# Attention in a fixed order on TensorE: longest score rows first, transposes in shared banks, convolution taps in another place

## The chip, the cores and the metric

The program runs on one core of a Trainium2 chip. A core has TensorE (PE in the profile, with its weight loads as PEld), VectorE (DVE), ScalarE (ACT), GpSimd (POOL) and SyncE (SP), which issues most transfers. The metric is the device time of one execution in microseconds (us). Three executions of the kernel before took 2982.3, 2982.48 and 2983.72 us, median 2982.48. A difference of 0.2% is 6 us.

## The reference

Two blocks run one after the other on 512 tokens of width 1024, all in 32-bit floats. The first is a gated delta rule with pooling; the change does not touch it. The second has two layers, and in each stand a feed-forward part, a mixer, a second feed-forward part and a gate. The change lies in the mixer:

```
z = u @ w_in
y_attn = forgetting_attention(q, k, v, f_logit) @ w_attn_out
y_conv = conformer_conv(glu_in, conv_w, conv_b, g_conv) @ w_conv_out
merged = sigmoid(z_a) * y_attn + sigmoid(z_c) * y_conv
return merged @ w_out
```

The attention has 8 heads of width 64, is causal over 512 tokens in blocks of 128 queries, and adds a running sum of log-sigmoids to the scores before the softmax. The convolution is a causal one over time, channel by channel, with 31 taps on 512 channels; behind it stand an RMS normalization over the channels and a SiLU.

## The kernel before

All activations lie transposed, 128 channels by 512 tokens to a tile. A product with a weight of 32 bits is made of three matmuls on rounded halves (`mm3`, L154 to L159): high weight by high activation, high by low, low by high. The weights come in a fixed order through a stream (`Stream`, L83): a transfer of eight 128x128 blocks, then for each four blocks a rounding on ScalarE (`whi`, L108) and a subtraction on VectorE (`wlo`, L109). There are three buffers for each half, and the stream is used strictly in its order, so a projection can't begin before the one ahead of it in the order has used its weights.

The mixer of a layer runs thus. Four `glu` blocks make the inputs of the convolution (`ca`), then come the values `vt` and the forget logits. Then `heads(hp, ...)` runs for four pairs of heads (the **heads stage** below). While a pair is worked on, a filler gives TensorE the projections of the next pair's queries and keys (`qk_steps`, 16 steps of three matmuls each), for the last pair the first of the 16 gates (`first_gates`, `GATES0`, 8 steps to a gate). For a block of 128 queries (`qb`) and each of the two heads there are two score matmuls and a mask matmul into a bank `sc` (L453, L455, L459), the maximum on VectorE (L461), the exponential on ScalarE (L463), a reciprocal and a scaling on VectorE (L464, L468). Then, for each block of keys (`kb`) and each head, the rows `pe` are transposed on TensorE (L478) into a bank `pt`, copied by VectorE (L482), and multiplied with the values into `o` (L486). `split` makes `oh` and `ol` of `o` (L169, L170).

The convolution is one VectorE operation for each tap and 128 channels, 4 x 31 = 124 in a layer (L415, L420). `taps(n)` writes n of them at the place where it is called: 12 behind each `glu` block, 8 behind the values, 5 in each pair of heads (`TAPS1`), 12 behind each attention output block (`TAPS2`).

After the heads, `part(i)` for i from 0 to 7 multiplies a block of the attention output with its gate, and from 8 to 15 a block of the convolution's output; the gate for i+3 is projected ahead of it (24 matmuls to a gate, 12 to a part). `conv_out` (L563) normalizes the convolution: squares on ScalarE, sums on VectorE, one matmul for the mean (`ssps`, L261), a square root on ScalarE, then a reciprocal and three more operations on VectorE (L252 to L256), a scaling (L575), a SiLU (L576) and a split into `yh` and `yl`, which part 8 is the first to read. It is written ahead of part `CONV_AT`.

What an engine does in which order is not what the code writes: when the program is built, a list scheduler fills each engine's list. It takes the earliest instruction in the code that is ready by its own estimate, and where nothing earlier is ready it takes a later one. At run time each engine goes through its list in that order. Four banks (`acc`) hold projections, four more (`aux`) hold scores, transposes, `o` and `ssps`.

Of the kernel before, what the change touches and what calls it, by code (L numbers as in the profile page):

```python
# [7 lines left out]
F32 = mybir.dt.float32  # L8
# [5 lines left out]
P = 128  # L14
S = 512
D = 1024
KD = D // P
# [3 lines left out]
GRP = 8  # L21
UNIT = 4
AHEAD = 3
ENG2 = dict(pe="v", dup="a", pt="vv")
BANKS2 = (4, 4)
TAPS0 = 12
TAPSV = 8
GATES0 = 1
FILL = (3, 4, 3, 0, 1, 2, 1, 2)
TAPS1 = (1, 1, 2, 1)  # L30
TAPS2 = 12
CONV_AT = 5
NEG = -float(2 ** 100)
EPS = 1e-6

# [142 lines left out]
def block2(tc, kk, W, h, xp, x0, sq0, p_t, par, out_t):  # L178


    nc = tc.nc
    with ExitStack() as ctx:
# [32 lines left out]
        maskr = cp.tile([P, P], F32R, name="maskr")  # L215
# [7 lines left out]
        xh, xl = x0  # L223
# [3 lines left out]
        def mtile(i, name, dt=F32R):  # L227
            return mp.tile([P, S], dt, tag=f"m{i}", name=name)
# [37 lines left out]
        def proj(name, l, col, ps=None, k_n=KD, x=None):  # L266
            ps = psum("pj") if ps is None else ps
            x = (xh, xl) if x is None else x
            for k in range(k_n):
                w = W.get((name, l, k * P, col))  # L270
                mm3(nc, ps, w, (x[0][k], x[1][k]), k == 0, k == k_n - 1)
            return ps

        def proj_steps(ps, name, l, col):
            for k in range(KD):
                mm3(nc, ps, W.get((name, l, k * P, col)), (xh[k], xl[k]), k == 0, k == KD - 1)
                yield

        def token_sums(sq):
# [82 lines left out]
        def mixer(l, after):  # L362
# [66 lines left out]
            def taps(n):  # L429

                while n > 0 and done[0] < 31 * len(ca):
                    next(conv)
                    done[0] += 1
                    n -= 1
                if done[0] == 124:
                    next(conv, None)

            def heads(hp, qk1, filler):

                rr = [slice(64 * i, 64 * i + 64) for i in range(2)]  # L440

                def fill(n):
                    for _ in range(n):
                        next(filler, None)

                pp = [[], []]
                for qb in range(4):
                    n = (qb + 1) * P
                    qs = slice(qb * P, qb * P + P)
                    pss = [paux("sc") for i in range(2)]  # L450
                    for i, ps in enumerate(pss):
                        q, k = qk1[i]
                        nc.tensor.matmul(ps[:, :n], lhsT=q[:, qs], rhs=k[:, :n], start=True, stop=False)  # L453
                        q, k = qk2[hp % 2][i]
                        nc.tensor.matmul(ps[:, :n], lhsT=q[:, qs], rhs=k[:, :n], start=False, stop=False)  # L455
                    fill(FILL[qb])
                    for i, ps in enumerate(pss):
                        o = ps[:, :n]
                        nc.tensor.matmul(ps[:, qs], lhsT=kk.identr, rhs=maskr, start=False, stop=True)  # L459
                        sm = sp.tile([P, 4], F32, tag="sm", name="sm", bufs=4)  # L460
                        nc.vector.tensor_reduce(sm[:, 0:1], o, axis=mybir.AxisListType.X, op=ALU.max, negate=True)  # L461
                        pe = cp.tile([P, n], F32, tag=f"pe{qb}", name="pe", bufs=2)
                        nc.scalar.activation(pe, o, AF.Exp, bias=sm[:, 0:1], accum_out=sm[:, 1:2])  # L463
                        nc.vector.reciprocal(sm[:, 2:3], sm[:, 1:2])  # L464
                        if ENG2["pe"] == "a":
                            nc.scalar.activation(pe, pe, AF.Copy, scale=sm[:, 2:3])
                        else:
                            nc.vector.tensor_scalar(pe, pe, sm[:, 2:3], None, op0=ALU.mult)  # L468
                        pp[i].append(pe)
                    taps(TAPS1[qb])  # L470
                po_ = paux("o")
                for kb in range(4):
                    n = S - kb * P
                    pts = []
                    for i in range(2):
                        ps = paux("pt")
                        for qb in range(kb, 4):
                            nc.tensor.transpose(ps[:, (qb - kb) * P:(qb - kb) * P + P], pp[i][qb][:, kb * P:kb * P + P],  # L478
                                                kk.ident)
                        t = mtile(8 + kb % 2 * 4 + 2 * i, "pt", F32)[:, :n]  # L480
                        copy = nc.scalar.copy if ENG2["pt"][i] == "a" else nc.vector.tensor_copy
                        copy(t, ps[:, :n])  # L482
                        pts.append(t)
                    fill(FILL[4 + kb])
                    for i, r in enumerate(rr):
                        nc.tensor.matmul(po_[r, kb * P:], lhsT=vt[kb][:, hp * P + 64 * i:hp * P + 64 * i + 64], rhs=pts[i],  # L486
                                         start=kb == 0, stop=kb == 3)
                split(nc, oh[hp], ol[hp], po_)

            for cb in range(4):  # L490
# [11 lines left out]
            for k in range(KD):  # L502
                wh, wl = W.get(("w_in_2", l, k * P, 1024), 4)
# [5 lines left out]
            vt = [mtile(t, f"vt{t}", F32) for t in range(4)]  # L509
# [20 lines left out]

            gates = []

            def gate_steps(i):
                pg = psum("pj")
                yield from proj_steps(pg, "w_in_2", l, 2568 + i * P)
                g = tmp("ga")
                nc.vector.tensor_tensor(g, pg, R, op=ALU.mult)
                nc.scalar.activation(g, g, AF.Sigmoid)
                gates.append(g)

            def gate(i):
                for _ in gate_steps(i):
                    pass

            def first_gates():
                for i in range(GATES0):
                    yield from gate_steps(i)

            qk1 = [], []
            for _ in qk_steps(0, qk1):  # L550
# [54 lines left out]
            for m in range(KD):  # L605
                ps = proj("w_out_2", l, m * P, x=(mh, ml))
# [37 lines left out]
        v = sp.tile([P, 4], F32, name="lv")  # L644
        r = sp.tile([P, 4], F32, name="lr")
# [3 lines left out]
        for m in range(KD):  # L649
            t = tmp("fin")  # L650
# [950 lines left out]
```

## Time and profile before

| | |
|---|---|
| median of three runs | 2982.48 us |
| the profiled execution | 2981.43 us, of it span 2979.7 us |
| PE busy | 2934.9 us (98%) |
| DVE busy | 1910.1 us (64%) |
| ACT busy | 1298.3 us (44%) |
| layer 1, heads stage, 1174.8 to 1267.7 us | 92.90 us: PE busy 89.50, DVE 83.90, ACT 52.76 |
| layer 1, 1267.7 to 1341.0 us, up to part 8 | 73.30 us: PE busy 73.30, DVE 62.44, ACT 33.10 |
| layer 2, heads stage and a little, 2292.2 to 2385.6 us | 93.40 us: PE busy 90.21, DVE 83.31, ACT 52.87 |

A row of the instruction view has the start, the duration, the engine, the line, the operation, what it writes and reads, and in brackets how long the engine stood idle before it and what ended that. A matmul's start is measured, its end is modelled, and one begins before the last has ended: the distance from start to start tells TensorE's pace. VectorE's operations overlap a little in the records too.

### The profile page before, as it was taken

How to read it: one execution, taken by the hardware profiler on the slowest of the kernel's cores; microseconds unless marked ns; L12 is line 12 of the kernel's file. 1: busy time of each engine (PE TensorE's matmuls, PEld its weight loads, DVE VectorE, ACT ScalarE, POOL GpSimd, SP SyncE). 2: the span in 40 equal slices, each digit the busy share in tenths (PEclk: the TensorE clock that was granted, in tenths of full speed). 3: DMA queues.
4: the chain of work that ended last, by engine and by line, in shares of the span. 5: the costliest groups of instructions: out<-in, count | busy, mean ns of one | idle time of the engine just before them, and what ended most of it. 6: DMA issues, size and time to landing. Idle time of an engine off the chain costs nothing.

```text
span 2979.7 us, 37937 instructions
## 1 busy us (share of the span) xinstructions
PE 2934.9 (98%) x13992; PEld 2392.2 (80%) x13992; DVE 1910.1 (64%) x3753; ACT 1298.3 (44%) x2387; POOL 48.1 (2%) x105
## 2 busy tenths in 40 slices
PE   8999999999999999999999999999999999999998
PEld 5888887778888887688888888888888688888886
DVE  6788888787544469886543447444469886543446
ACT  6567766435323335544432335323335544432333
POOL 1000000000000000000000000000000000000000
PEclk9999999999999999999999999999999999999999
DMA  5211123233233332123333333333232123233332
GB/s 216 57 42 47 45 58 106 92 92 92 92 99 98 94 99 85 50 85 99 94 98 99 96 95 102 97 99 98 94 99 84 50 87 99 92 99 98 94 99 85
DMA packets 112986, 268.77 MB, mean 90 GB/s; under 512 B 43552, under 2 KB 47136, under 8 KB 112800
## 3 DMA queue, kind: packets, MB, share of 16 engines
q1 hardware_dynamic: 111776, 266.28, 28.8%
q8 instruction: 110, 1.80, 0.2%
q14 instruction: 76, 0.62, 0.1%
q0 software_dynamic: 1024, 0.07, 0.0%
HBM read 262.17 MB, written 4.06 MB: 89 GB/s over the span
## 4 chain that ended last, share of the span: by engine, by line
PE 93%; DVE 3%; ACT 2%; issue 1%; DMA 0%; SPq 0%; DVEq 0%; ACTq 0%
PE pj L158 17%; PE pj L157 17%; PE pj L159 17%; PE fo L158 5%; PE fo L157 5%; PE fo L159 5%; PE px L157 3%; PE px L158 3%; PE px L159 2%; PE o L486 1%; PE wo L158 1%; PE mX L1285 1%; PE wo L159 1%; PE mP L1290 1%; PE wo L157 1%; PE chn L1337 1%
## 5 line engine op out<-in xcount | busy, mean ns | idle before, releaser
L108 ACT CAST whi<-wraw 128x512 fp32r<-128x512 f32 x914 | 567.1, 621 | 1163.9 <-PE pj L158 699.3
L109 DVE TENSOR_TENSOR wlo<-wraw,whi 128x512 fp32r<-128x512 f32 x914 | 627.3, 687 | 446.1 <-ACT whi L108 423.6
L158 PE MATMUL pj<-xl,whi 128*128 128x512 f32 x1712 | 672.6, 393 | 0.0
L157 PE MATMUL pj<-xh,whi 128*128 128x512 f32 x1712 | 670.5, 392 | 0.9 <-DVE h L1526 0.9
L159 PE MATMUL pj<-xh,wlo 128*128 128x512 f32 x1712 | 669.3, 391 | 0.0
L159 PEld LDWEIGHTS pj<-xh,wlo 128*128 128x128 f32 x1712 | 321.9, 188 | 67.9 <-issue 2.3
L158 PEld LDWEIGHTS pj<-xl,whi 128*128 128x128 f32 x1712 | 322.2, 188 | 66.9 <-issue 2.7
L157 PEld LDWEIGHTS pj<-xh,whi 128*128 128x128 f32 x1712 | 322.2, 188 | 66.4 <-ACT whi L108 1.3
L157 PE MATMUL fo<-gh,whi 128*128 128x512 f32 x704 | 273.9, 389 | 0.0
L158 PE MATMUL fo<-gl,whi 128*128 128x512 f32 x704 | 273.9, 389 | 0.0
L159 PE MATMUL fo<-gh,wlo 128*128 128x512 f32 x704 | 273.9, 389 | 0.0
L420 DVE SCALAR_TENSOR_TENSOR cy<-ca,par,cy 128x489 f32<-128x489 f32 (+17 forms) x240 | 169.6, 729 | 1.5
L157 PE MATMUL px<-xh,whi 128*128 128x512 f32 x392 | 160.3, 409 | 0.8 <-ACT xh L1000 0.7
L158 PE MATMUL px<-xl,whi 128*128 128x512 f32 x392 | 160.6, 410 | 0.0
L159 PE MATMUL px<-xh,wlo 128*128 128x512 f32 x392 | 159.1, 406 | 0.0
L157 PEld LDWEIGHTS fo<-gh,whi 128*128 128x128 f32 x704 | 132.1, 188 | 27.5
L159 PEld LDWEIGHTS fo<-gh,wlo 128*128 128x128 f32 x704 | 132.1, 188 | 27.5
L158 PEld LDWEIGHTS fo<-gl,whi 128*128 128x128 f32 x704 | 132.1, 188 | 27.4
L341 DVE TENSOR_TENSOR fb<-pj,R 128x512 f32<-128x512 f32 x88 | 60.8, 691 | 129.9 <-PE pj L159 129.9
L338 DVE TENSOR_TENSOR fa<-pj,R 128x512 f32<-128x512 f32 x88 | 60.8, 691 | 125.4 <-PE pj L159 123.5
L157 PE MATMUL pj<-nh,whi 128*128 128x512 f32 x352 | 137.3, 390 | 0.0
L158 PE MATMUL pj<-nl,whi 128*128 128x512 f32 x352 | 137.0, 389 | 0.0
(427 smaller groups left out, 4473.4 us busy)
## 6 DMA issues: line engine op xcount, KB each, us to landing
wraw<-in_w_dram SPq DMA_DIRECT2D x465, 512.0 KB
mw<-in_w_dram SPq DMA_DIRECT2D x16, 512.0 KB
raw<-in_xt_dram SPq DMA_DIRECT2D x8, 256.0 KB
h<-in_xt_dram SPq DMA_DIRECT2D x8, 256.0 KB
out_dram<-fin SPq DMA_DIRECT2D x8, 256.0 KB
db<-B SPq DMA_DIRECT2D x64, 6.0 KB
Pm<-dq SPq DMA_DIRECT2D x64, 12.0 KB
Qm<-dq SPq DMA_DIRECT2D x64, 12.0 KB
```

What stands on the lines that cost most here:

```text
L108: nc.scalar.copy(hi, src)
L109: nc.vector.tensor_tensor(lo, src, hi.bitcast(F32), op=ALU.subtract)
L157: nc.tensor.matmul(ps, lhsT=wh, rhs=xh, start=start, stop=False)
L158: nc.tensor.matmul(ps, lhsT=wh, rhs=xl, start=False, stop=False)
L159: nc.tensor.matmul(ps, lhsT=wl, rhs=xh, start=False, stop=stop)
L338: nc.vector.tensor_tensor(a, pa, R, op=ALU.mult)
L341: nc.vector.tensor_tensor(b, pb, R, op=ALU.mult)
L420: nc.vector.scalar_tensor_tensor(yy[:, s:], ca[cb][:, :S - s], pcol("conv_w", l, cb, j), yy[:, s:], op0=ALU.mult, op1=ALU.add)
L486: nc.tensor.matmul(po_[r, kb * P:], lhsT=vt[kb][:, hp * P + 64 * i:hp * P + 64 * i + 64], rhs=pts[i], start=kb == 0, stop=kb == 3)
L1285: nc.tensor.matmul(pX[:, o], lhsT=st.B[:, m0 + m], rhs=alt(st.Q, m0 + m), start=True, stop=True)
L1290: nc.tensor.matmul(pP[:, o], lhsT=Xt[:, m], rhs=alt(st.P, m0 + m), start=True, stop=True)
L1337: nc.tensor.matmul(pa, lhsT=st.kN[:, c], rhs=y2, start=True, stop=True)
```

## The change

Scores: the query blocks go from the last (512 keys) to the first (128 keys), and the three matmuls of a head stand together, with the filler's steps behind each block (`FILL`). Softmax: the scaling of the second head's rows moves to ScalarE (`ENG2`). Transposes: five batches instead of eight, each filling a bank of 512 columns, copied in turn by VectorE and ScalarE; three batches, two filler steps, the values of key block 0, two batches, two filler steps, and the values of key blocks 1 to 3, both heads each time. All these matmuls, and the filler's, are marked to stay in the order in which the code writes them (`keep_in_program_order`). The calls of `taps` inside `heads` are gone, `conv_out` is written ahead of part 7 instead of part 5, and the last pair has two gates as its filler instead of one. No transfer is added, taken away or moved: the lists of POOL and SP are the same.

```diff
-ENG2 = dict(pe="v", dup="a", pt="vv")
+ENG2 = dict(pe="va", dup="a", pt="vavav")
-GATES0 = 1
-FILL = (3, 4, 3, 0, 1, 2, 1, 2)
-TAPS1 = (1, 1, 2, 1)
+GATES0 = 2
+FILL = (2, 2, 3, 5, 2, 2)
-CONV_AT = 5
+CONV_AT = 7
...
+        def pin(*a, **kw):
+            tc.keep_in_program_order(nc.tensor.matmul(*a, **kw))
...
-                for qb in range(4):
+                for qi, qb in enumerate((3, 2, 1, 0)):
...
-                        if ENG2["pe"] == "a":
+                        if ENG2["pe"][i] == "a":
...
-                    taps(TAPS1[qb])
+                    fill(FILL[qi])
+                banks = (((0, 0),), ((1, 0),), ((0, 1), (0, 3)), ((1, 1), (1, 3)), ((0, 2), (1, 2)))
+                def transposes(j):
+                    ps = paux("pt")
+                    t = mtile(8 + (5 * hp + j) % 8, "pt", F32)
...
+                    copy = nc.scalar.copy if ENG2["pt"][j] == "a" else nc.vector.tensor_copy
+                    copy(t[:, :at], ps[:, :at])
+                def values(kb):
+                    for i, r in enumerate(rr):
+                        pin(po_[r, kb * P:], lhsT=vt[kb][:, hp * P + 64 * i:hp * P + 64 * i + 64], rhs=pts[kb][i],
+                            start=kb == 0, stop=kb == 3)
+                for j in range(3):
+                    transposes(j)
+                fill(FILL[4])
+                po_ = paux("o")
+                values(0)
+                for j in range(3, 5):
+                    transposes(j)
+                fill(FILL[5])
+                for kb in range(1, 4):
+                    values(kb)
```

**TensorE's list, the values of the first pair of heads in layer 1.** `pj` is a projection of the filler, `pt` a transpose, `o` a product with the values. Before:

```order
L486 MATMUL o<-pt,vt_10929 64x512 x2
L478 MATMUL pt<-ident,pe 128x128 x8
L159 MATMUL pj<-xh_10175,wlo 128x512
L157 MATMUL pj<-xh_10233,whi 128x512
L158 MATMUL pj<-xl_10234,whi 128x512
L486 MATMUL o<-pt,vt_10930 64x384
L478 MATMUL pt<-ident,pe 128x128 x2
L159 MATMUL pj<-xh_10233,wlo 128x512
L486 MATMUL o<-pt,vt_10930 64x384
```

And now:

```order
L276 MATMUL o<-pt,vt_10929 64x512 x2
L488 MATMUL pt<-ident,pe 128x128 x8
L276 MATMUL pj<-xh_10347,whi 128x512
L276 MATMUL pj<-xl_10348,whi 128x512
L276 MATMUL pj<-xh_10347,wlo 128x512
L276 MATMUL pj<-xh_10399,whi 128x512
L276 MATMUL pj<-xl_10400,whi 128x512
L276 MATMUL pj<-xh_10399,wlo 128x512
L276 MATMUL o<-pt,vt_10930 64x384 x2
L276 MATMUL o<-pt,vt_10931 64x256 x2
L276 MATMUL o<-pt,vt_10932 64x128 x2
L276 MATMUL sc<-qk_11295,qk_11204 128x512
```

The two heads' products of a key block now stand side by side, in two runs to a pair instead of six, and the next pair's scores come right behind the second.

**VectorE's list, the end of the first pair of heads in layer 1.** `cy` is a tap of the convolution, `ol` the low half of the pair's output, with which a pair ends. Before:

```order
L109 TENSOR_TENSOR wlo<-wraw,whi 128x512
L482 COPY pt<-pt 128x384
L482 COPY pt<-pt 128x256 x2
L482 COPY pt<-pt 128x128
L420 SCALAR_TENSOR_TENSOR cy<-ca,par_80,cy 128x482
L482 COPY pt<-pt 128x128
L420 SCALAR_TENSOR_TENSOR cy<-ca,par_80,cy 128x504
L415 TENSOR_SCALAR cy<-ca,par_80 128x512
L170 TENSOR_TENSOR ol_10419<-o,oh_10415 128x512
```

And now:

```order
L109 TENSOR_TENSOR wlo<-wraw,whi 128x512
L493 COPY pt<-pt 128x512 x2
L427 SCALAR_TENSOR_TENSOR cy<-ca,par_80,cy 128x500
L427 SCALAR_TENSOR_TENSOR cy<-ca,par_80,cy 128x510
L427 SCALAR_TENSOR_TENSOR cy<-ca,par_80,cy 128x499
L427 SCALAR_TENSOR_TENSOR cy<-ca,par_80,cy 128x509
L493 COPY pt<-pt 128x512
L427 SCALAR_TENSOR_TENSOR cy<-ca,par_80,cy 128x498
L109 TENSOR_TENSOR wlo<-wraw,whi 128x512
L384 SCALAR_TENSOR_TENSOR qk<-pj,R 128x512
L427 SCALAR_TENSOR_TENSOR cy<-ca,par_80,cy 128x497
L170 TENSOR_TENSOR ol_10419<-o,oh_10415 128x512
```

The scheduler has set taps between the copies; over the four pairs of a layer, from behind the first pair's last `qk` scaling to the last `ol`, the list holds 59 taps where it held 26, and behind that none, where it held 33.

**TensorE's list, from the mean of the convolution's squares to part 8.** `ssps` is that mean, the rows with `xh` and `xl` are a gate, `yh` is what part 8 reads. Before, the list from the mean on began thus:

```order
L261 MATMUL ssps<-ysq,ones_74 128x512
L158 MATMUL pj<-xl_10234,whi 128x512
L159 MATMUL pj<-xh_10233,wlo 128x512
L157 MATMUL pj<-xh_10289,whi 128x512
L158 MATMUL pj<-xl_10290,whi 128x512
```

And now it ends thus ahead of part 8:

```order
L159 MATMUL pj<-xh_10289,wlo 128x512
L157 MATMUL pj<-xh_10347,whi 128x512
L158 MATMUL pj<-xl_10348,whi 128x512
L159 MATMUL pj<-xh_10347,wlo 128x512
L157 MATMUL pj<-xh_10399,whi 128x512
L158 MATMUL pj<-xl_10400,whi 128x512
L159 MATMUL pj<-xh_10399,wlo 128x512
L157 MATMUL pj<-yh_12520,whi 128x512
L158 MATMUL pj<-yl_12524,whi 128x512
```

Between the mean and the first matmul with `yh` stood 83 matmuls (the rest of a gate, part 6, a gate, part 7, a gate); now there stand 11, the rest of one gate. Layer 2 has the same lists.

## Rows read from the trace of the kernel before

**Rows 1.** Page, busy time, share and instructions of each engine.

```profile
PE 2934.9 (98%) x13992; PEld 2392.2 (80%) x13992; DVE 1910.1 (64%) x3753; ACT 1298.3 (44%) x2387; POOL 48.1 (2%) x105
```

**Rows 2.** Stretches: length; busy PE, PEld, DVE, ACT, POOL (instructions); PEclk, DMA, GB/s.

```profile
1175.70:1269.10 93.40, 90.56 (x435) 61.87 (x436) 83.83 (x198) 53.05 (x118) 3.83 (x8) 0.98 0.18 52
1267.70:1341.00 73.30, 73.30 (x323) 60.11 (x322) 62.44 (x93) 33.10 (x52) 0.00 (x0) 1.00 0.28 87
2292.20:2385.60 93.40, 90.21 (x426) 61.44 (x424) 83.31 (x197) 52.87 (x118) 4.47 (x10) 0.96 0.17 52
```

**Rows 3.** VectorE by line, 1175.7 to 1269.1: busy, mean ns, idle before.

```profile
L420 DVE SCALAR_TENSOR_TENSOR cy<-ca,par,cy 128x485 f32<-128x485 f32 (+24 forms) x25 | 17.9, 724 | 0.1
L482 DVE COPY pt<-pt 128x512 f32<-128x512 f32 (+3 forms) x32 | 14.5, 485 | 4.2 <-PE pt L478 3.9
L468 DVE TENSOR_SCALAR pe<-pe,sm 128x128 f32<-128x128 f32 (+3 forms) x32 | 11.3, 379 | 0.0
L170 DVE TENSOR_TENSOR ol<-o,oh 128x512 fp32r<-128x512 f32 x4 | 2.8, 690 | 1.9 <-ACT oh L169 1.9
```

**Rows 4.** The same with shapes apart, the widest copy.

```profile
L482 DVE COPY pt<-pt 128x512 f32<-128x512 f32 x8 | 5.3, 683 | 0.3
```

**Rows 5.** TensorE in order of time, where the heads stage begins.

```profile
1174.53 0.39 PE L157 MATMUL pj<-xh,whi 128*128 128x512 f32 x1
1174.76 0.39 PE L158 MATMUL pj<-xl,whi 128*128 128x512 f32 x1
1177.15 0.33 PE L453 MATMUL sc<-qk,qk 128*128 128x128 f32 x1 [2.01 <-ACT qk L395]
```

**Rows 6.** TensorE in order of time, products with the values (two records each).

```profile
1196.10 0.86 PE L486 MATMUL o<-pt,vt 128*64 128x384 f32 x2
...
1263.98 0.87 PE L486 MATMUL o<-pt,vt 128*64 128x384 f32 x4
...
1267.33 0.44 PE L486 MATMUL o<-pt,vt 128*64 128x128 f32 x4
```

**Rows 7.** TensorE in order of time, the convolution's mean and part 8.

```profile
1321.41 1.10 PE L261 MATMUL ssps<-ysq,ones 128*128 128x512 f32 x2
1321.94 0.80 PE L158 MATMUL pj<-xl,whi 128*128 128x512 f32 x1
1322.58 0.40 PE L159 MATMUL pj<-xh,wlo 128*128 128x512 f32 x1
...
1341.21 0.39 PE L157 MATMUL pj<-yh,whi 128*128 128x512 f32 x1
```

**Rows 8.** VectorE in order of time, from the mean to the scaled outputs.

```profile
1323.72 3.35 DVE L253 RECIPROCAL R<-rs 128x512 f32<-128x512 f32 x1 [1.31 <-ACT rs L252]
1326.99 0.63 DVE L109 TENSOR_TENSOR wlo<-wraw,whi 128x512 fp32r<-128x512 f32 x1
...
1331.57 0.68 DVE L256 SCALAR_TENSOR_TENSOR R<-rs,R 128x512 f32<-128x512 f32 x1
1332.17 0.68 DVE L586 TENSOR_TENSOR ma<-pj,ga 128x512 f32<-128x512 f32 x1
1332.77 1.40 DVE L575 SCALAR_TENSOR_TENSOR cy<-cy,par,R 128x512 f32<-128x512 f32 x2
```

**Rows 9.** ScalarE in order of time, the same stretch.

```profile
1323.00 0.69 ACT L252 ACTIVATE rs<-ssps,epsb 128x512 f32<-128x512 f32 x1
...
1335.01 1.15 ACT L576 ACTIVATE cy<-cy 128x512 f32<-128x512 f32 x2
...
1336.58 1.14 ACT L169 CAST yh<-cy 128x512 fp32r<-128x512 f32 x2
```

**Rows 10.** Stretches behind the wait of rows 5, columns as in rows 2.

```profile
1178.00:1180.00 2.00, 1.61 (x11) 1.57 (x10) 1.97 (x5) 1.67 (x2) 0.00 (x0) 0.75 0.78 262
1180.00:1182.00 2.00, 2.00 (x8) 1.81 (x7) 2.00 (x9) 1.86 (x8) 0.00 (x0) 0.50 0.00 0
2299.00:2301.00 2.00, 2.00 (x7) 1.85 (x6) 1.83 (x8) 2.00 (x7) 0.00 (x0) 0.50 0.01 4
```

More of the change, by code (lines that the diff above doesn't have):

```diff
@@ L272, in proj @@
             return ps
+        def pin(*a, **kw):
+            tc.keep_in_program_order(nc.tensor.matmul(*a, **kw))
         def proj_steps(ps, name, l, col):
             for k in range(KD):
-                mm3(nc, ps, W.get((name, l, k * P, col)), (xh[k], xl[k]), k == 0, k == KD - 1)
+                (wh, wl), x = W.get((name, l, k * P, col)), (xh[k], xl[k])
+                pin(ps, lhsT=wh, rhs=x[0], start=k == 0, stop=False)
+                pin(ps, lhsT=wh, rhs=x[1], start=False, stop=False)
+                pin(ps, lhsT=wl, rhs=x[0], start=False, stop=k == KD - 1)
                 yield
@@ L444, in fill @@
                         next(filler, None)
-                pp = [[], []]
-                for qb in range(4):
+                pp = [[None] * 4, [None] * 4]
+                for qi, qb in enumerate((3, 2, 1, 0)):
                     n = (qb + 1) * P
                     qs = slice(qb * P, qb * P + P)
-                    pss = [paux("sc") for i in range(2)]
-                    for i, ps in enumerate(pss):
+                    for i in range(2):
+                        ps = paux("sc")
+                        o = ps[:, :n]
                         q, k = qk1[i]
-                        nc.tensor.matmul(ps[:, :n], lhsT=q[:, qs], rhs=k[:, :n], start=True, stop=False)
+                        pin(o, lhsT=q[:, qs], rhs=k[:, :n], start=True, stop=False)
                         q, k = qk2[hp % 2][i]
[L455 to L459, printed above, removed]
+                        pin(o, lhsT=q[:, qs], rhs=k[:, :n], start=False, stop=False)
+                        pin(ps[:, qs], lhsT=kk.identr, rhs=maskr, start=False, stop=True)
                         sm = sp.tile([P, 4], F32, tag="sm", name="sm", bufs=4)
@@ L468, in heads @@
                             nc.vector.tensor_scalar(pe, pe, sm[:, 2:3], None, op0=ALU.mult)
-                        pp[i].append(pe)
-                    taps(TAPS1[qb])
-                po_ = paux("o")
[L472 to L487, printed above, removed]
+                        pp[i][qb] = pe
@@ new lines, in heads @@
+                    fill(FILL[qi])
+                pts = [[None, None] for _ in range(4)]
+                banks = (((0, 0),), ((1, 0),), ((0, 1), (0, 3)), ((1, 1), (1, 3)), ((0, 2), (1, 2)))
+                def transposes(j):
+                    ps = paux("pt")
+                    t = mtile(8 + (5 * hp + j) % 8, "pt", F32)
+                    at = 0
+                    for i, kb in banks[j]:
+                        n = S - kb * P
+                        for qb in range(kb, 4):
+                            o = at + (qb - kb) * P
+                            tc.keep_in_program_order(nc.tensor.transpose(ps[:, o:o + P], pp[i][qb][:, kb * P:kb * P + P],
+                                                                         kk.ident))
+                        pts[kb][i] = t[:, at:at + n]
+                        at += n
+                    copy = nc.scalar.copy if ENG2["pt"][j] == "a" else nc.vector.tensor_copy
+                    copy(t[:, :at], ps[:, :at])
@@ L531, in mixer, with open_gate @@
             gates = []
-            def gate_steps(i):
-                pg = psum("pj")
-                yield from proj_steps(pg, "w_in_2", l, 2568 + i * P)
+            def open_gate(pg):
                 g = tmp("ga")
@@ L541, in gate @@
             def gate(i):
-                for _ in gate_steps(i):
-                    pass
+                open_gate(proj("w_in_2", l, 2568 + i * P))
             def first_gates():
+                pgs = []
                 for i in range(GATES0):
-                    yield from gate_steps(i)
+                    pgs.append(psum("pj"))
+                    yield from proj_steps(pgs[i], "w_in_2", l, 2568 + i * P)
+                for pg in pgs:
+                    open_gate(pg)
             qk1 = [], []
```

## The prediction

> **What bounds the kernel now.** I read the page's first part first: TensorE is busy for 98% of the span and VectorE for 64% [rows 1]. So what counts is where TensorE waits or works slowly, and whether the change makes it wait anew. Then the stretches of one mixer [rows 2]. From 1267.7 us, behind the heads, to 1341.0 TensorE is busy for all of 73.30 us: nothing can be won there, only lost. In the heads stage VectorE is busy for 83.83 of 93.40 us, 90%, far more than its share of the span. TensorE has one long wait there, 2.01 us for ScalarE at the start of the first pair [rows 5]. So the heads stage is a place where two engines stand close to their limits, and a change that relieves TensorE wins only as far as VectorE follows. Then VectorE by line in the stage [rows 3], for what the change takes from it and gives to it; then, in order of time, the chain from the mean of the convolution's squares to part 8 on TensorE, VectorE and ScalarE [rows 7 to 9]; last the granted clock behind a wait [rows 10].
>
> **The heads stage, TensorE's side.** The number of score, mask, transpose and value matmuls stays, and so does that of projections, but for the second gate, which comes earlier and is missing later: no work is added. What becomes cheaper is the pairing of the two heads. One head's product of 384 columns took 0.86 us alone; where both heads' stood side by side, the two together took 0.87 [rows 6]. In the list before, 6 of a layer's 16 products stand apart (in the first pair of heads those of 384 and 128 columns), 1664 columns in all, 1664/384 x 0.86 = 3.7 us; now all 16 stand side by side. TensorE was idle for 2.84 us [rows 2], 2.01 of them in rows 5, so 0.8 us of other waits may go. That is 4.5 us in each layer; what the fewer changes between kinds of matmuls save has no row of its own, and I let it be as much again at most, so 4.5 to 9 us. The wait at the start stays: the first pair's queries and keys come no sooner.
>
> **The heads stage, VectorE's side.** This decides. From behind the first pair's last query and key scaling to the last `ol` VectorE's list held 197 instructions and now holds 193. Taken away: 32 copies at a mean of 0.485 us, 15.5 us, for which 12 of full width at 0.683 come, 8.2 [rows 3, 4], so -7.3; 16 of 32 scalings at 0.379 [rows 3], -6.1; one weight subtraction, -0.6 [rows 8]. Added: 59 - 26 = 33 taps at 0.724 [rows 3], +23.9. Sum: +9.9 us. The taps that the code puts behind the heads stand, in the list that the scheduler made, inside them, since it fills every moment in which it believes VectorE idle.
>
> VectorE was busy for 83.83 us in this stretch [rows 2], so it now has 93.7 us of work there, as much as the whole stage lasted. What TensorE needs of it is the last copy of transposes in the fourth pair, five rows ahead of the end (a tap, a weight subtraction, a gate, a tap, `ol`): they are 5 x 0.61 = 3.0 us, leaving 90.7. Without a single idle moment this copy is done at 1175.7 + 90.7 = 1266.4. The last products with the values follow, three pairs of at most 0.87 us [rows 6], about 1.7 us: 1268.1. Before, the last ones ended with the row at 1267.33, and TensorE's next matmul started at 1267.70 [rows 2, 6]. By then it now has done five projections more, 5 x 0.227 = 1.1 us by the distance of the starts in rows 5. So with VectorE never idle the stage is 0.7 us better than before. It won't be idle never: it waited 9.6 us of 93.40, of that 3.9 for transposes and 1.9 for `oh` [rows 2, 3]. The copies are now fewer and later, the wait for `oh` stays; I take 1.7 us of idle time, near the second figure. That gives **+1.0 us in a layer**.
>
> The ends: busy time counts the last 0.08 us of each operation even where the next starts later (a 0.68 us operation starts 0.60 behind its like [rows 8]), which may make 3.3 us, so -4; and if it stands idle as long as before, 9.6 us, +8.9. The nearest row is the wait for `oh`, hence +1.0.
>
> ScalarE gets 16 scalings and 8 copies, at 0.6 us at most 14 us on 53.05 [rows 2], 67 of 93: it can follow, and I put nothing for it.
>
> **Part 8 and the convolution's norm.** In the list before, 83 matmuls, 18.8 us, stand between the mean of squares and the first matmul with `yh`; that first one starts 19.8 us behind the mean, without an idle moment [rows 7]. Now 11 stand there. Count from the mean's start, T. TensorE: the next matmuls start at T + 0.53 and T + 1.17 [rows 7], ten more distances of 0.227 end at T + 3.4, where part 8 wants to start. The chain: square root at T + 1.59 [rows 7, 9]; reciprocal at T + 2.31, and what follows on VectorE 3.27 us later, T + 5.58 [rows 8]. In the new list a weight subtraction, an operation, a gate's product and two operations come there, at 0.60 each and 0.67 where one needs the one before: the first scaled output starts at T + 8.7, is done at T + 9.4, and ScalarE's SiLU starts at T + 9.5. Two SiLUs take 1.1 us, the rounding to `yh` 0.6 [rows 9]: part 8 starts at T + 11.2. TensorE stands idle for 7.8 us. Then it is paced by the rest: two more SiLUs and roundings, and the four `yl`, put the last operand at T + 14.6, part 8 ends at T + 15.1 instead of T + 6.2. **Loss: 8.9 us in a layer**, and nothing gives it back, since TensorE is full before and behind.
>
> The ends: without the weight subtraction and the gate in VectorE's chain 7.3 us; with the chain as slow as before (`yh` first rounded by 1337.2, T + 15.8 [rows 7, 9]) 13.
>
> **The clock.** After the wait of 2.01 us [rows 5] the granted clock fell to 0.75 and then 0.50 of full while TensorE was busy for 2.00 of 2.00 us, so to the lower of its levels, 1.2 of 2.4 GHz; in layer 2, whose stage begins ahead of 2292.2 [rows 2], it was 0.50 between 2299 and 2301 with TensorE busy throughout [rows 10]. Part 8's 12 matmuls at half pace cost 12 x 0.227 = 2.7 us more, of which about 1.2 lie inside the waits for `yl`. I add **1.5 us in a layer** (0 to 3).
> [...]
>
> **The other edits.** The reversed order of query blocks frees the banks of the long rows late and those of the short ones early; behind each block stand 6 to 15 projections, 1.4 to 3.4 us, and the banks come free with the exponentials, about as long after the scores: nothing. No transfer moves. The second gate needs a second projection bank, of four, while no other is wanted: nothing.
>
> **Sum.** For each layer +1.0 + 8.9 + 1.5 = 11.4 us, for two +22.8. The profiled execution took 2981.43 us (its span 2979.7 and 1.7 around it), the median is 1.05 above it. 2981.4 + 22.8 = 3004.2, at the median's level **3005 us**, 0.8% slower.
>
> **Rivals.**
> *TensorE sets the heads' pace (not slower).* The taps fit into moments in which VectorE idles, and TensorE wins its whole 9 us in each layer. For it: TensorE waited little in the stage, and the scheduler, too, laid the taps into idle moments of its own reckoning. Against it: even with the distances shortened as far as the -4 above allows, VectorE has no room for more than half. With -9 + 10.4 a layer is 1.4 us slower: 2985, no measurable change; with the low end of the wait at part 8 (7.3, no clock) it is 1.7 faster, 2979. It decides from 4 us in a layer.
> *The chain to part 8 is hidden.* Part 8's wait would need cover that the list doesn't hold. TensorE would have to take other matmuls first, against its list. Then +1.0 to -4 in a layer: 2984 to 2974.
> *More waits and a colder clock.* VectorE as the bound leaves TensorE idle in each heads stage for the 4.5 to 9 us that it saves, in small pieces, while it waits for weights and copies; if the clock is low for 15 us more of the stage and VectorE idles as much as before, a layer costs up to 8.9 + 8.9 + 3 = 21: 3018 to 3025.
> *The change doesn't do what it says.* Half of this is in the forecast already: the taps are not behind the heads.
>
> **Chances.** Forecast (2993 to 3015) 0.68; colder and more idle 0.15; TensorE's pace 0.11; chain hidden 0.06. The range for 8 in 10 runs from 2989, where the -4 in the heads and 7.3 at part 8 meet (2 x 3.3 and the median's level), to 3019. Faster or slower means by over 0.2%, 6 us, about what a measurement of this kernel can tell from no change: faster 0.05, same 0.10 (most of the first rival and half of the second), slower 0.85.
>
> **What would show it.** Part 8: a gap of about 8 us on TensorE right ahead of the first matmul with `yh`, ended by ScalarE's `yh`, in both layers, with the granted clock at 0.50 behind it; without it the forecast is wrong by 20 us. Heads: VectorE busy for over 92% from the first score to the last `ol`, TensorE waiting for VectorE's weight halves and copies several times in each pair, the two heads' products side by side in all 16 places. If TensorE's heads stage ends more than 4 us earlier than before, VectorE was not the bound there. Outside the mixers nothing should differ.

## The result and the profile after

The changed kernel took 3019.06 us (median of four executions, 3016.27 to 3020.72) against 2982.74 for the kernel before in the same comparison: ratio 1.0121, interval 1.0109 to 1.0133, 36 us slower. Forecast were 3005 us and a range of 2989 to 3019. The direction was right, the size was 1.6 times the forecast, and the time lies at the range's end (3019.06 against 3019). The profiled execution, the slowest of the four, took 3020.72 us, 39.3 more than the profiled one before; 1.8 of that stand ahead of the first mixer.

The page's busy line, to be held against [rows 1]:

```profile
PE 2934.8 (97%) x13992; PEld 2402.0 (80%) x13992; DVE 1887.7 (63%) x3681; ACT 1317.0 (44%) x2431; POOL 48.1 (2%) x105
```

TensorE's busy time is the same to 0.1 us. All the loss is idle time or work at half pace that replaced work at full pace elsewhere. TensorE's waits over the whole program (waiter, what released it, us in total, times, longest):

```profile
PE sc L276 <- ACT qk L402: 24.7, 14, 6.5
PE pj L157 <- ACT yh L169: 17.6, 2, 8.8
```

The first was 4.6 us in all before the change, the second did not exist. The stretches that answer to [rows 2], from the first score to behind the last product with the values, first in layer 1 before the change, then in layers 1 and 2 after it, and from there to the mean of the convolution's squares:

```profile
1177.15:1267.70 90.55, 89.16 (x430) 60.69 (x430) 81.57 (x194) 51.20 (x115) 3.83 (x8) 0.98 0.18 53
1178.93:1273.97 95.04, 87.59 (x437) 66.01 (x437) 89.98 (x189) 59.77 (x136) 3.83 (x8) 0.94 0.16 45
2315.92:2410.78 94.86, 87.45 (x438) 65.78 (x438) 90.08 (x189) 59.77 (x136) 3.83 (x8) 0.94 0.15 45
1273.97:1346.70 72.73, 72.73 (x322) 59.98 (x320) 31.77 (x49) 25.30 (x42) 0.00 (x0) 1.00 0.31 95
```

VectorE is busy for 95% of the heads stage and TensorE idle for 7.5 us of it; before, for 1.4. In the dense stretch nothing is lost, and VectorE has little to do there now. TensorE in order of time, where the stage begins (answers to [rows 5]) and where the second and third pairs of heads begin:

```profile
1172.00 0.39 PE L276 MATMUL pj<-xh,wlo 128*128 128x512 f32 x1
1178.93 0.79 PE L276 MATMUL sc<-qk,qk 128*128 128x512 f32 x1 [6.54 <-ACT qk L402]
...
1203.45 0.50 PE L276 MATMUL sc<-qk,qk 128*128 128x512 f32 x1 [2.02 <-ACT qk L402]
...
1228.49 0.50 PE L276 MATMUL sc<-qk,qk 128*128 128x512 f32 x1 [1.84 <-ACT qk L402]
```

The first score stands no later than before, 44.9 us behind the layer's first matmul of the values in both. But 20 projections that TensorE did ahead of it before are now held behind it, so the wait is 4.5 us longer. Each later pair's first scores wait for the last split of keys by ScalarE (the fourth pair's for 1.4 us). The way there on VectorE and on ScalarE at the end of the first pair:

```profile
1199.58 0.68 DVE L493 COPY pt<-pt 128x512 f32<-128x512 f32 x1
1200.18 0.73 DVE L427 SCALAR_TENSOR_TENSOR cy<-ca,par,cy 128x498 f32<-128x498 f32 x1
1200.82 0.68 DVE L109 TENSOR_TENSOR wlo<-wraw,whi 128x512 fp32r<-128x512 f32 x1
1201.42 0.68 DVE L384 SCALAR_TENSOR_TENSOR qk<-pj,R 128x512 f32<-128x512 f32 x1
```

```profile
1202.14 0.62 ACT L389 CAST qk<-qk 64x512 fp32r<-64x512 f32 x1
1202.78 0.62 ACT L402 CAST qk<-qk 64x512 fp32r<-64x512 f32 x1
```

The keys' last projection matmul had started at 1199.60; a tap and a weight subtraction stand ahead of its scaling, then come two casts. Between the projection and the scores TensorE's fixed list has only six products with the values (two records each).

At part 8 (answers to [rows 7 to 9]), TensorE, VectorE and ScalarE:

```profile
1346.74 1.10 PE L261 MATMUL ssps<-ysq,ones 128*128 128x512 f32 x2
...
1349.97 0.39 PE L159 MATMUL pj<-xh,wlo 128*128 128x512 f32 x1
1359.16 0.79 PE L157 MATMUL pj<-yh,whi 128*128 128x512 f32 x1 [8.80 <-ACT yh L169]
...
1364.74 0.63 PE L157 MATMUL pj<-xh,whi 128*128 128x512 f32 x1
```

```profile
1349.04 3.35 DVE L253 RECIPROCAL R<-rs 128x512 f32<-128x512 f32 x1 [1.31 <-ACT rs L252]
...
1355.50 2.74 DVE L598 SCALAR_TENSOR_TENSOR cy<-cy,par,R 128x512 f32<-128x512 f32 x4
```

```profile
1354.21 1.28 ACT L558 ACT_TABLE_LOAD   x1 [3.43 <-DVE ga L557]
1355.51 0.63 ACT L558 ACTIVATE ga<-ga 128x512 f32<-128x512 f32 x1
1356.15 1.28 ACT L599 ACT_TABLE_LOAD   x1
1357.45 1.15 ACT L599 ACTIVATE cy<-cy 128x512 f32<-128x512 f32 x2
1358.51 1.12 ACT L169 CAST yh<-cy 128x512 fp32r<-128x512 f32 x2
```

With T = 1346.74 the scaling starts at T + 8.76 as forecast (T + 8.7). The SiLU starts at T + 10.71 instead of T + 9.5: the gate's sigmoid stands ahead of it on ScalarE, and each of the two has a table load of 1.28 us. The sigmoid is through when the first scaled output is ready, at about 1356.15; the SiLU's own load, from 1356.15 to 1357.43, is what the chain gained. Part 8 is followed at T + 18.0; forecast were T + 15.1 and 1.5 us of clock. Its twelve matmuls, most of them started 0.43 us apart where 0.227 is usual, ran at the lower level, as the clock column says (stretches behind the wait at part 8 and behind the three waits ahead of scores shown above):

```profile
1359.10:1364.00 4.90, 4.84 (x11) 3.53 (x12) 2.59 (x4) 2.61 (x6) 0.00 (x0) 0.50 0.00 0
1178.93:1182.00 3.07, 3.07 (x8) 2.29 (x9) 2.95 (x5) 2.86 (x4) 0.00 (x0) 0.50 0.00 0
1204.00:1207.00 3.00, 2.82 (x8) 2.18 (x9) 2.89 (x5) 1.50 (x5) 0.00 (x0) 0.65 0.00 0
1229.00:1232.00 3.00, 2.62 (x12) 2.01 (x13) 2.86 (x5) 1.50 (x5) 0.00 (x0) 1.00 0.02 5
```

**One measure for all runs.** Kernels differ in how many projections TensorE has done by the end of the heads. So I take the time from a layer's first matmul of the values (`vt`) to the last product with them, less 0.2275 us for each projection matmul in between: the *heads' cost*. Before, layer 1: from 1132.22 to 1267.49 with 281 projections, 135.27 - 63.93 = 71.3. After: from 1134.00 to 1273.77 with 269, 139.77 - 61.20 = 78.6. The same way from the mean to the first matmul with `yh` less the projections between is 0.9 before and 9.9 after: the wait at part 8 costs 9.0. From there to the next norm's mean, less the projections, it is -0.2 before and 3.1 after: 3.3 more, part 8 at half pace.

The measure holds the clock too. The changed kernel and e2 below run the same instructions in the same order in the heads, and layer 2 costs 78.4 and 80.3 (mean granted clock of the stage 0.94 and 0.91); so do e4 and e5, and layer 1 costs 68.5 and 66.7 (0.96 and 1.00). A difference of under 2 us between two runs therefore says nothing about their lists.

### The profile page after: what moved, and what is told of

Its sections match the earlier page's. It is cut to its first block, busy times and chain, and to the rows that moved or that the text cites. A ratio compares the mean times of both kernels' runs of the same rounds, so it can differ in the third digit from the quotient of the medians.

```text
span 3019.0 us, 37821 instructions
## 1 busy us (share of the span) xinstructions
PE 2934.8 (97%) x13992; PEld 2402.0 (80%) x13992; DVE 1887.7 (63%) x3681; ACT 1317.0 (44%) x2431; POOL 48.1 (2%) x105
## 4 chain that ended last, share of the span: by engine, by line
PE 93%; DVE 3%; ACT 3%; issue 1%; DMA 0%; SPq 0%; DVEq 0%; ACTq 0%
PE pj L157 16%; PE pj L158 16%; PE pj L159 16%; PE fo L157 5%; PE fo L159 5%; PE fo L158 5%; PE pj L276 3%; PE px L157 3%; PE px L158 3%; PE px L159 2%; PE wo L158 1%; PE mX L1308 1%; PE wo L159 1%; PE sc L276 1%; PE mP L1313 1%; PE wo L157 1%
## 5 line engine op out<-in xcount | busy, mean ns | idle before, releaser
L158 PE MATMUL pj<-xl,whi 128*128 128x512 f32 x1552 | 607.2, 391 | 0.0
L157 PE MATMUL pj<-xh,whi 128*128 128x512 f32 x1552 | 605.0, 390 | 0.9 <-DVE h L1549 0.9
L159 PE MATMUL pj<-xh,wlo 128*128 128x512 f32 x1552 | 604.1, 389 | 0.0
L159 PEld LDWEIGHTS pj<-xh,wlo 128*128 128x128 f32 x1552 | 291.4, 188 | 62.8 <-issue 2.3
L158 PEld LDWEIGHTS pj<-xl,whi 128*128 128x128 f32 x1552 | 291.6, 188 | 62.0 <-issue 1.9
L157 PEld LDWEIGHTS pj<-xh,whi 128*128 128x128 f32 x1552 | 291.6, 188 | 61.8 <-ACT whi L108 1.3
L427 DVE SCALAR_TENSOR_TENSOR cy<-ca,par,cy 128x489 f32<-128x489 f32 (+21 forms) x240 | 169.5, 729 | 1.0
```

The costliest lines, as they stand in the source:

```text
L427: nc.vector.scalar_tensor_tensor(yy[:, s:], ca[cb][:, :S - s], pcol("conv_w", l, cb, j), yy[:, s:], op0=ALU.mult, op1=ALU.add)
```

## The experiments

All times are medians; the kernel before took 2980.8, 2981.5 and 2981.9 us beside the three groups of runs (e1 to e4, e5 to e8, e9 to e12). Heads' costs are those of layers 1 and 2.

| run | us | ratio to before, interval | heads' cost | PE idle ahead of part 8 |
|---|---|---|---|---|
| before | 2982.7 | | 71.3, 72.6 | none |
| after | 3019.1 | 1.0109 to 1.0133 | 78.6, 78.4 | 8.8 |
| e1 before, norm ahead of part 7 | 3004.4 | 1.0066 to 1.0096 | 71.4, 71.7 | 8.8 |
| e2 after, norm ahead of part 5 | 2998.4 | 1.0042 to 1.0072 | 78.5, 80.3 | none |
| e3 after, taps held behind the heads | 3006.5 | 1.0068 to 1.0098 | 72.0, 71.7 | 9.3 |
| e4 after, filler 8 steps ahead | 2997.7 | 1.0040 to 1.0074 | 68.5, 68.5 | 8.8 |
| e5 e4 and norm ahead of part 5 | 2973.0 | 0.9964 to 0.9983 | 66.7, 66.7 | none |
| e6 e5 and taps dealt out | 2995.7 | 1.0030 to 1.0059 | 79.1, 79.2 | none |
| e7 after, no marks, norm ahead of part 5 | 2965.9 | 0.9930 to 0.9960 | 65.4, 63.7 | none |
| e8 before, `ENG2` shared | 2978.3 | 0.9978 to 0.9996 | 70.4, 70.2 | none |
| e9 after, no marks | 2993.9 | 1.0023 to 1.0049 | 67.1, 65.2 | 8.8 |
| e10 e7 with filler ahead | 2969.9 | 0.9949 to 0.9975 | 66.0, 66.0 | none |
| e11 e7, short rows first | 2971.1 | 0.9957 to 0.9980 | 67.4, 67.0 | none |
| e12 e7, VectorE alone | 2970.7 | 0.9948 to 0.9974 | 66.0, 65.2 | none |

**e1 and e2: part 8 alone.** The kernel before with `-CONV_AT = 5` `+CONV_AT = 7`, and the changed kernel with the opposite edit.

> The kernel before with one number changed: the convolution's norm is written ahead of part 7 instead of part 5. TensorE's list then has 11 matmuls between the mean of squares and part 8, as in the changed kernel, and 83 stood there before; the heads are as before. Theory (part 8's wait is a loss of its own, with nothing to pay it back): in each layer 9.0 us of waiting ahead of part 8, as between the two profiled executions, and 3.2 us for part 8 at the lower clock, 12.2 a layer, 2982.7 + 24.4 = 3007 us. Rival (the wait needs the changed heads, since they push the convolution's end): the wait is under 3 us and the time under 2990.

> The changed kernel with the convolution's norm written ahead of part 5 again; 83 matmuls stand between the mean and part 8. Theory (two losses that add up): part 8's 12.2 us a layer go, the heads keep theirs, 7.2 us in layer 1 and 5.8 in layer 2: 3019.1 - 24.4 = 2995 us, with 6.5 us of waiting ahead of the first score and three waits of about 2 us ahead of the other pairs' first scores as they were. Rival (the wait at part 8 comes from VectorE being late out of the heads, so it stays): above 3010. Rival that the heads cost nothing by themselves: 2983.

Measured: +23.6 us and -20.7. In e1 TensorE's longest new wait is the same as in the changed kernel, with heads like those before:

```profile
1349.33 0.79 PE L157 MATMUL pj<-yh,whi 128*128 128x512 f32 x1 [8.79 <-ACT yh L169]
```

Against the kernel before that ran beside each, e1 lost 23.6 us and e2 17.6. Together that is 41.2 where the changed kernel lost 36.3, so the two losses add up to within 5 us; 1.9 of the 5 are the clock in e2's second layer. Part 8 costs 9 to 12 us a layer by itself, and the heads the rest.

**e3: VectorE without taps in the heads.**

```diff
-                    taps(TAPS2)
+                    with tc.issue_after(last[0].ins):   # last: the last pair's `ol` on VectorE
+                        taps(TAPS2)
```

The `taps(200)` ahead of the norm is held in the same way.

> The changed kernel with all taps that the code writes behind the heads held behind the last pair's low half on VectorE: 0 taps in the heads stage instead of 56, 68 behind it instead of 0. Theory V (VectorE's work holds the heads): without 56 x 0.725 = 40 us VectorE is no longer full; the three waits of about 2 us ahead of the pairs' first scores shrink below 1 us, and the heads stage from the first score to the last product falls from 95 us to 85 to 90. Theory O (the fixed order holds them: a pair's first scores stand right behind the projection that its keys come from, so the wait is the latency of scaling, split and copy whatever VectorE has beside it): the three waits stay at 1.5 to 2.2 us, the stage shrinks by less than 3 us. In both the wait ahead of part 8 stays or grows (2 matmuls of cover instead of 11, VectorE with 68 taps there): 9 to 14 us a layer. Time by V 2998 to 3012, by O 3015 to 3025.

Measured: 3006.5 us, the heads' cost down by 6.6 and 6.7. The time (2998 to 3012) and the length of the stage (85 to 90 us) are those of theory V, and theory O's were missed; but of the waits at the pairs, which by V go below 1 us each, 5.2 of 5.8 us in layer 1 are left. The stage:

```profile
1177.18:1266.96 89.78, 84.40 (x436) 65.13 (x436) 59.03 (x133) 61.80 (x137) 4.00 (x9) 0.94 0.15 48
```

VectorE is down to 59 of 90 us, yet TensorE still waits for ScalarE's keys at each pair, now 0.64 and 1.09 us for the two heads (1.7 together; 2.02 and 0.18 at the second pair of the changed kernel). So taking the taps out, which make each answer of VectorE later, won back most of what the heads had lost (72.0 and 71.7 are left, the kernel before had 71.3 and 72.6). But with not one tap in the stage the waits at the pairs are still there: they belong to the order.

**e4 and e5: the keys projected earlier.**

```diff
+            def ahead():
+                for hp in range(1, 4):
+                    yield from qk_steps(hp, nxt[hp])
+                yield from first_gates()
+            filler = ahead()
+            for _ in range(8):
+                next(filler)
```

All pairs share this filler, `FILL` is (2, 2, 3, 3, 2, 2); e5 has `CONV_AT = 5` too.

> The changed kernel with the filler made one stream that runs 8 steps ahead: 24 projections of the second pair stand ahead of the first score, and each pair's keys are projected half a pair before its first scores; matmuls in fixed order as before, norm ahead of part 7 as in the changed kernel. Theory O: the waits ahead of the pairs' first scores (4.5 us more than before at the first, three of about 2 us) go, and the half-paced stretches behind them; 6 to 10 us a layer, 2999 to 3007 us. Theory V: VectorE's list is nearly as long (47 taps in the stage instead of 56), so TensorE's idle time in the stage only moves to other waits (copies of transposes, weights) and stays over 5 us; what is won is the start and 9 taps, 3 to 5 us a layer, 3009 to 3013. In both the wait of about 9 us ahead of part 8 stays.

> The run with the leading filler and, besides, the norm ahead of part 5 again. Theory (the two losses add up): part 8's wait of 9.0 us and its half-paced matmuls, 2.8, go in each layer: 2997.7 - 23.6 = 2974 us, below the kernel before. Rival (without the wait at part 8 VectorE's work of the convolution is late elsewhere): 2978 to 2985.

Measured: 2997.7 and 2973.0 us. Theory O's figure was exceeded: 10 us a layer, with 47 taps still in the stage. The waits ahead of later pairs' first scores are gone. But theory V's sign came true as well: TensorE's idle time moved to other waits, now ahead of the transposes for the scaled rows, and was 6.5 us in e4's stage and 7.4 in e5's. The stages of the two, and the longest waits in e4's:

```profile
1176.29:1263.79 87.50, 80.98 (x425) 61.38 (x425) 83.43 (x178) 61.56 (x138) 3.84 (x8) 0.96 0.16 49
1176.58:1262.28 85.70, 78.31 (x425) 59.00 (x425) 83.23 (x178) 61.46 (x138) 3.84 (x8) 1.00 0.16 50
```

```profile
PE pt L489 <- DVE pe L474: 2.8, 1, 2.8
PE pt L489 <- ACT pe L472: 2.4, 2, 2.2
```

Of the 10 us in layer 1, 24 x 0.2275 = 5.5 are projections done ahead of a first score that came no later, and 0.9 less idle time; the rest is matmuls that took less time, at a mean granted clock of 0.96 instead of 0.94. With the early norm it beats the kernel before.

**e6: the taps dealt out.** e5 with two taps behind each block of scores, held behind the maximum of the block's second head (`red` is the last one set), the rest held behind the heads:

```diff
                     fill(FILL[qi])
+                    with tc.issue_after(red.ins):
+                        taps(2)
```

> The same with the taps dealt out: 2 behind each block of scores and held behind the first maximum (32 taps in the heads stage instead of 47), the other 36 held behind the last pair, and only 56 instead of 67 ahead of the first score. Theory V (VectorE's work still sets the stage's length with the leading filler): the first score comes 1.8 us sooner, as with the taps held behind, and 2 to 3 us more go in the stage: 7 to 10 us less than the run with leading filler and early norm, 2964 to 2967. Theory O (the order was the cause and the lead has settled it): within 4 us of that run, 2970 to 2976.

Both theories missed: 2995.7 us, 22.7 slower than e5, with fewer taps in the stage (32 for 47). The stage, and TensorE's waits in it:

```profile
1173.67:1273.00 99.33, 84.00 (x424) 64.03 (x424) 75.13 (x165) 61.19 (x138) 4.01 (x8) 0.91 0.13 43
```

```profile
PE pt L492 <- DVE pe L475: 9.7, 2, 5.2
PE pt L492 <- ACT pe L473: 3.1, 1, 3.1
```

VectorE is busy for 76%, and TensorE is idle for 15.3 us, more than in any other run. The taps, which by their place in the code now come ahead of work written later, stand between a row's maximum and its scaling; in the second pair, ahead of the wait of 5.2 us, there are eight of them. In the first pair:

```profile
1184.97 0.40 DVE L468 TENSOR_REDUCE sm<-sc 128x1 f32<-128x256 f32 x1
1185.29 0.71 DVE L428 SCALAR_TENSOR_TENSOR cy<-ca,par,cy 128x484 f32<-128x484 f32 x1
1185.92 0.41 DVE L468 TENSOR_REDUCE sm<-sc 128x1 f32<-128x256 f32 x1
1186.26 0.15 DVE L471 RECIPROCAL sm<-sm 128x1 f32<-128x1 f32 x1
1186.33 0.70 DVE L428 SCALAR_TENSOR_TENSOR cy<-ca,par,cy 128x483 f32<-128x483 f32 x1
1186.95 0.34 DVE L475 TENSOR_SCALAR pe<-pe,sm 128x256 f32<-128x256 f32 x1
```

So the amount of VectorE's work doesn't decide by itself: what stands ahead of the one operand that the fixed list needs next can cost more than a smaller amount saves.

**e7 and e9: the marks taken off.**

```diff
         def pin(*a, **kw):
-            tc.keep_in_program_order(nc.tensor.matmul(*a, **kw))
+            nc.tensor.matmul(*a, **kw)
```

The same for the transposes. e7 has `CONV_AT = 5`, e9 has 7 and is the changed kernel but for the marks.

> The changed kernel without the marks that hold TensorE's order (the code's order, banks and engines as in the changed kernel) and with the norm ahead of part 5. TensorE's list has 20 projections ahead of the first score again, 36 taps stand in the heads stage instead of 56. If the fixed order is what costs in the heads, their cost falls by 6 to 8 us a layer, to that of the kernel before: 2998.4 - 14 = 2984 us. If the order of the rows and the shared banks cost, whatever holds them: 2994 to 3000. If these gain and only the fixed order loses: below 2977.

> The changed kernel with the marks that hold TensorE's order taken off and nothing else; the norm stays ahead of part 7, with 11 matmuls between the mean and part 8. If the marks' loss and part 8's add up, it takes what the unmarked kernel with the early norm took and 11.8 us more in each layer: 2965.9 + 23.6 = 2989.5 us. If the gain in the heads were eaten by the convolution, which now has 21 taps behind the heads, the wait ahead of part 8 would be longer than 9.0 us and the time above 2995.

Measured: 2965.9 us for e7, the fastest of all, 0.55% below the kernel before; its third case came true. The stage, and TensorE's waits in it:

```profile
1175.01:1255.50 80.49, 78.90 (x410) 59.60 (x412) 77.11 (x168) 58.57 (x136) 3.84 (x8) 0.96 0.16 53
```

```profile
PE sc L276 <- ACT qk L402: 2.0, 1, 2.0
PE o L276 <- DVE pt L492: 0.9, 2, 0.8
```

VectorE is busy for 77.11 of 80.49 us, 96%, a larger share than after the change, and TensorE idles for 1.6. Its list holds 36 taps in the stage where the changed kernel's held 56, 77 us of work for 90. The products of the two heads stand side by side here too. e9, which differs from the changed kernel by the marks alone, is 25 us faster than it, and its heads' cost is 11.5 and 13.2 lower. It is 4.4 us above its figure, between its two cases; the wait at part 8 is the same 8.8 us, and 3.2 of the 4.4 are in the heads, with the lists of e7 there.

**e8 and e10 to e12: what else is in it.** e8 is the kernel before with `ENG2 = dict(pe="va", dup="a", pt="va")` and `ENG2["pe"][i]`. The others are e7 with the stream of e4, with `enumerate((0, 1, 2, 3))`, and with `ENG2 = dict(pe="vv", dup="a", pt="vvvvv")`.

> The kernel before with the second head's scalings and copies of transposes on ScalarE instead of VectorE, nothing else (no fixed order; the scheduler sets 41 taps into the heads stage instead of 23, and 15 instead of 33 behind it). If VectorE's work sets the pace of the heads stage before the change, TensorE's wait there shrink and it is 4 to 8 us faster, 2973 to 2977. If not (VectorE stood idle for 9.6 us of that stage, and TensorE for 1.4 behind the first score), it is within 3 us of the kernel before, 2978 to 2984; more taps in the stage eat what the scalings leave.

> The unmarked kernel with the norm ahead of part 5 and, besides, the filler as one stream 8 steps ahead. If the lead only repairs what the fixed order spoils (a pair's keys projected right ahead of its first scores), nothing is left for it here: 2963 to 2969 us. If the lead has a worth of its own (the wait of 2.0 us ahead of the first score goes, and the half-paced stretch behind it), 2 to 4 us a layer more: 2958 to 2962.

> The unmarked kernel with the norm ahead of part 5, but the score rows from the shortest to the longest, as in the kernel before. If the order of the rows is worth nothing: within 4 us of 2965.9. If a good part of what this kernel has over the one before (15.6 us) is the order of the rows: 2972 or more, with TensorE waiting for the exponentials of the last, longest rows ahead of the first transposes.

> The unmarked kernel with the norm ahead of part 5, but all scalings and copies on VectorE, as before the change: 16 scalings and 8 copies a layer, some 11.6 us, go back to it, and the scheduler sets 21 taps instead of 36 into the heads stage. If relieving VectorE is what wins: 4 to 6 us a layer are lost, 2974 to 2978. If the shared banks and the products side by side win: within 4 us of 2965.9, since the taps make room.

Measured: 2978.3, 2969.9, 2971.1 and 2970.7 us. e8 wins 3.2 us, at the edge of its second case. It doesn't show what less work on VectorE is worth, since the scheduler set taps in the place of the scalings and VectorE was as busy as before (82.2 us in the stage for 81.6). No gain from the lead is seen without the marks (1 us above the range of its first case). e11 and e12 lie between their two cases. In the heads' cost the order of the rows makes 2.0 and 3.3 us a layer and the sharing with ScalarE 0.6 and 1.5, less than the 6 and 9 that e7 has over the kernel before, but hardly more than the 2 us that the clock can make, and the intervals of e10, e11 and e12 overlap that of e7. What is left is owed to what these runs share: the banks, the products side by side, the second gate, the other places of filler and taps. None was undone alone, so their shares stay open.

## Why the prediction was right in direction and short in size

*Part 8 and the norm: the mechanism right, 2 us short in a layer.* Forecast were 8.9 us, of them 7.8 idle ahead of part 8 and 1.1 waits inside it, and 1.5 of clock, 10.4 in all. Measured are 9.0 ahead of it and 3.3 inside (3.2 in layer 2), 12.3 in all. The chain came as worked out up to the scaled output; the idle time was 8.8 instead of 7.8 us, since the table load ahead of the SiLU was not in the sum. The kernel before had it there too (from 1333.72), and [rows 8, 9] show that the SiLU began 1.5 us behind the first scaled output and not 0.1. Part 8 itself waited hardly at all for `yl`, but all twelve matmuls and the next ones ran at half pace: the estimate that 1.2 of 2.7 us would lie inside other waits was wrong. The granted clock was 0.50 behind this wait, 0.65 behind the wait of 2.02 us and 1.00 behind that of 1.84. The Trainium skill ("TensorE: Matmul & The Clock Gate", section "HAM oscillation — how this bites in real kernels") describes a kernel in which each burst follows a wait for a transfer of about 3 to 5 us and starts cold. The trace agrees for the wait of 8.8 us; the two shorter waits are outside what that kernel shows.

*The heads: +1.0 was the wrong term; measured +7.2 in layer 1 and +5.8 in layer 2.* The step that failed is "By then it now has done five projections more". In the trace 269 projections are done by the last product instead of 281, twelve fewer: eight more in the stage, but 20 fewer ahead of the first score. That is 17 x 0.2275 = 3.9 us in each layer. The prediction took the wait at the start for unchanged because the queries and keys come no sooner; it did not ask what TensorE did while it waited. The remainder, 2.3 and 0.9 us, was not taken apart further: it is what the waits for the next pairs' keys and the half-paced matmuls behind them cost beyond the 1.7 us of idle time in the sum and what the pairing won. The layers differ by the clock of the kernel before, 0.98 and 0.96 in the two stages [rows 2], where it is 0.94 in both after the change.

*VectorE as the bound: the row came true, the cause only in part.* VectorE was busy for 95% of the stage, as forecast ("over 92%"), and its taps did hold TensorE up: without them (e3) the heads cost 6.6 us less. But the busy share doesn't show a bound: in e7 it is 96%, at a heads' cost 13 to 15 us lower, and in e6 76%, at a cost as high as in the changed kernel. The taps are work that the scheduler sets into the time that it reckons free, 56 in this stage and 36 in e7, so taking off the marks also took work from VectorE here, and how much of the gain is owed to that was not separated. The waits that I expected, for weights and copies "several times in each pair", were 1.5 us in a layer, for copies alone; the waits that came were for keys. What e3, e4 and e9 show is that the marks hold TensorE at operands that are late, and that taps on VectorE make them later. Freeing VectorE won 6.6 us, projecting earlier 10, taking off the marks alone 11.5 to 13 (e9); they overlap.

*TensorE's side, 4.5 to 9 us to be won: there to be had, and given away.* e7 has it: 71.34 - 65.38 = 6.0 and 72.6 - 63.7 = 8.9, the second with help of the clock (1.00 in that stage, 0.96 before). That it comes from the pairing, as the forecast had it, no run shows. The gain needs none of the marks.

*The rivals.* The third, more waits and a colder clock, had 3018 to 3025, and the time is there: its mechanism (idle pieces in the heads and a low clock behind them) was part of what happened, its reason (VectorE's pace) only in part. That the time still lies at the end of the range is owed to the range's width, not to the heads' term. That part 8 is hidden, or that TensorE sets the pace of the changed heads, is refuted by the waits.

*The sum.* For the profiled executions: heads 7.2 + 5.8, part 8's wait 2 x 9.0, its clock 3.3 + 3.2, together 37.5 us; from the first matmul of the values in layer 1 to that in layer 2 the changed kernel took 19.5 us longer, and from there to the end 18.0. Of the 14.7 us missing in the 22.8, 11.0 are the heads' and 3.7 part 8's.

## What to carry to other kernels

Before an engine's order is fixed, look at which instructions the free order had put into its waits: here fixing the order of the waiting work was harmless, and fixing the filler's took the cover away. The program with the filler alone freed and the norm ahead of part 5 was not run, but as built it has the very lists of e7 on every engine, so once the filler is free the marks on scores, transposes and values do nothing. An engine that is 95% busy is not thereby the bound, if part of its work could stand elsewhere; ask what stands in its queue ahead of the operand that is waited for. And a chain of small steps behind one result needs its cover counted in matmuls: 11 behind the mean cost 12 us a layer, 83 cost nothing.

## What was not expected of the hardware

- Two waits of the same kind and nearly the same length (2.02 us before 1203.45, 1.84 us before 1228.49) had different sequels: the granted clock was 0.65 in one stretch behind and 1.00 in the other (rows above). In e5 TensorE was idle for 7.4 of 85.7 us, up to 2.7 us at a time, and the granted clock stayed 1.00 throughout the stage.
- Behind the wait of 8.8 us thirteen matmuls ran at half pace, 1359.16 to 1365.17, though TensorE was busy all that time.
- ScalarE loads a table for the sigmoid and another for the SiLU, 1.28 us each, ahead of part 8; the second stands on the chain to it.
